# Output projection's first part: the gate scaled by ScalarE on the way out of PSUM, the residual added by a DMA

## The chip, the cores and the metric

The kernel runs on one core of a Trainium2 chip. Its engines have queues of their own: TensorE (PE in the profile, its weight loads PEld), VectorE (DVE), ScalarE (ACT), GpSimd (POOL) and SyncE (SP), which only issues transfers. The metric is the device time of one execution in microseconds, as the median of several runs; less is better.

## The reference, cut to what matters

Two layers run over 640 tokens: 512 latent tokens and 128 context tokens, which have modulation vectors of their own. The part at issue is the gated residual after the mixer:

```
sh1, sc1, gt1, sh2, sc2, gt2 = _modulation(c, w_ada[l], b_ada[l])
h = _rms_norm(xs, g_mix[l]) * (1.0 + sc1) + sh1
mix = _mixer_latent(h, ...)              # concat of window attention, Fourier mixing, latent attention
xs = xs + gt1 * (mix @ w_out[l])
h = _rms_norm(xs, g_ffn[l]) * (1.0 + sc2) + sh2
xs = xs + gt2 * _conv_ffn(h, w_ug[l], conv_w[l], conv_b[l], w_down[l])
```

The context tokens go the same way with `c_ctx`.

## The kernel before, in words

Activations lie transposed: the residual is 8 chunks of 128 features by 640 tokens, a chunk to a tile `x` of 320 KB. Each matmul in float32r is done three times (high times high, low times high, high times low), so weights and activations are split into a high part, made by ScalarE (`wh`, `mh`, `CK`, ...: line 125), and a low part, made by VectorE (`wl`: line 188, `ml` and the like: line 144).

A layer is a mixer (projections, attention, output projection) and a feed-forward part, whose matmuls are dense. In the mixer, attention units run in a pipeline, and a generator called `filler` gives TensorE other work between them, in an order written by hand in `CFG[l]["order"]`: projections, the Fourier part, the parts of the latent attention, the modulation vectors of layer 0 (`early`, `ada`) and the steps `po0` to `po3`. The order on each engine is then set by a scheduler from this program order; an engine runs its own list strictly in order.

`po0` to `po3` are the first part of the output projection, two chunks each. The generator `part1` multiplies those input features that are ready early (4 of 8 blocks, or 6 of 8 for `po3` of layer 1) and leaves residual plus gated partial sum in DRAM, in `xpart[l]`. For that it loads the old residual chunk into a tile `xp` from `xsrc` (the input `xT` in layer 0, the buffer `xd` in layer 1), lets VectorE add the gated product in PSUM to it (`resid`, line 537: three instructions a chunk, over 320, 192 and 128 columns, since the two kinds of token have gates of their own), and stores it. `gate` is a copy of one column by GpSimd, which holds back what GpSimd issues next.

`pre_tail`, called with the fourth latent-attention unit, loads the eight sums from `xpart` into the tiles `x`; these loads stand behind the last store on GpSimd's queue. The second part multiplies the blocks left over and adds them to `x` with `resid`, whose `x` rows begin a layer's last mixer stretch; then the feed-forward part follows.

Three resources around this matter. PSUM has two large accumulators (the pool `pmm`, tiles `mm`) and four small ones (`pss`, tiles `s`). `part1` uses a large one for chunks 0 to 3 and small ones for 4 to 7 (`wide`); the attention scores, the key projection `knope` and others use the large ones too, in turn. SBUF tiles of most kinds come from one pool of 54 buffers. Weight tiles `wr` have two buffers (`NWR`): unit i+2 is loaded by SP when unit i has been split, that is, after its `wl` row on VectorE. The blocks `wa` of the modulation matrix are loaded by SP as well (line 301) and multiplied at line 320; the sums go through ScalarE (`adasb`) and a transpose (line 330).

```
            self.nsp = i + 1
            self.load_to(i + 2)
```

Of the kernel before, what the change touches and what calls it, by code (L numbers as in the profile page):

```python
# [10 lines left out]
AF = mybir.ActivationFunctionType  # L11
ALU = mybir.AluOpType
# [9 lines left out]
HF = 320  # L22
# [51 lines left out]
def segs(hf):  # L74
    return [(0, 320, 0)] if hf == 0 else [(320, 512, 0), (512, 640, 1)]
# [3 lines left out]
def hybrid_step(ctx: ExitStack, tc: tile.TileContext, I, O):  # L79
    nc = tc.nc  # L80
# [9 lines left out]
    def S(name, dt=F32, w=NT):  # L90
        return sp.tile([128, w], dt, tag="S", name=name)
# [23 lines left out]
    def SM(name, w=4, bufs=4):  # L115
        return sm.tile([128, w], F32, tag=name, name=name, bufs=bufs)
# [137 lines left out]
    mod = [const.tile([128, 48, 2], F32, name=f"mod{l}") for l in range(L)]  # L254
    amod = [const.tile([128, 2, 8, 2], F32, name=f"amod{l}") for l in range(L)]
    xd = dr.tile([8, 128, NT], F32, name="xd")
    xpart = [dr.tile([8, 128, NT], F32, name=f"xpart{l}") for l in range(L)]
# [15 lines left out]
    def dense(w, hs, ks, ps, first, last, hfs=(0, 1), off=0, n=NT, fix=False):  # L273
        for k in ks:
            for pi, (wi, hi) in enumerate(((0, 0), (0, 1), (1, 0))):
                for hf in hfs:
                    c0, c1 = hf * HF, n if hf else HF
                    pin(nc.tensor.matmul(  # L278
                        ps.h[hf][:, :c1 - c0], lhsT=w[wi][:, off[k] if isinstance(off, dict) else k + off, :], rhs=hs[hi][k][:, c0:c1],
                        start=(first and k == ks[0] and pi == 0), stop=(last and k == ks[-1] and pi == 2),  # L280
                    ), fix)
            yield 0.41 * len(hfs)
# [250 lines left out]
    def resid(xc, ps, l, gidx, c, hfs):  # L533
        for hf in hfs:
            for c0, c1, v in segs(hf):
                o = c0 - hf * HF
                nc.vector.scalar_tensor_tensor(  # L537
                    out=xc[:, c0:c1], in0=ps.h[hf][:, o:o + c1 - c0], scalar=mod[l][:, gidx * 8 + c, v:v + 1],
                    in1=xc[:, c0:c1], op0=ALU.mult, op1=ALU.add)
# [108 lines left out]
    def gate(t):  # L648

        g = SM("gate", 1)  # L650
        last_gate[0] = nc.gpsimd.tensor_copy(g, t)

    def gated(ins):
        if last_gate[0] is not None:
            tc.keep_in_program_order(ins)
        return ins
# [14 lines left out]
    def mixer(l, norm, begun, xsrc):  # L671
# [261 lines left out]
        def part1(i):  # L933
            late = i in CFG[l]["late"]
            while st["a"] < (10 if late else 5):
                yield 1e9
            for c in (2 * i, 2 * i + 1):
                xt = S("xp")
                gated(nc.gpsimd.dma_start(out=xt, in_=xsrc[c]))
                ps = Acc(c < CFG[l]["wide"])  # L940
                n = 6 if late else 4
                yield from dense(W.get(u["o", c if late else 2 * i]), (mh, ml), KORD[:n], ps, True, True, off={k: j + (0 if late else n * (c % 2)) for j, k in enumerate(KORD[:n])})
                resid(xt, ps, l, 2, c, (0, 1))
                nc.gpsimd.dma_start(out=xpart[l][c], in_=xt)
                gate(xt[:, 0:1])
                yield 0.0

        def filler():
            mla()
            parts = dict(fourier=fourier(*dft), q2=one("q2", cb_q(2)), q3=one("q3", cb_q(3)), kv=kv(), k1=k1())  # L950
            parts.update(zip(("ckv", "cqA", "cqB", "rest"), st["parts"]))
            parts.update({f"po{i}": part1(i) for i in range(4)})
            early = ada_pe(l, (4, 5) if l == 0 else (), CFG[l]["ahead"][0])
            ada = ada_pe(l, range(6, 10) if l == 0 else (), CFG[l]["ahead"][1])
            for n in CFG[l]["order"].split():
                if n == "load":
                    next(ada, None)
                elif n in ("early", "ada"):
                    yield from ada_chunk(early if n == "early" else ada)
                else:  # L960
                    if n == "ckv":
                        rope_load("ropeC")
                    yield from parts[n]
            for v in ada:
                yield max(v, 0.0)
# [219 lines left out]
        xn = {}  # L1185
        def pre_tail():
            for c in range(8):
                xn[c] = S("x")
                gated(nc.gpsimd.dma_start(out=xn[c], in_=xpart[l][c]))

        def pre_g1():
            while 7 not in Q:
# [26 lines left out]
        for c in range(8):  # L1219
            ps = Acc()  # L1220
# [8 lines left out]
    if True:  # L1229
# [22 lines left out]
        for l in range(L):  # L1252
# [8 lines left out]
            xn, nrm = mixer(l, nrm, begun, I["xT"] if l == 0 else xd)  # L1261
# [70 lines left out]
            for kind, a in u["plan"]:  # L1332
                if kind == "up":
                    for q, cb in (("a", cb_a(a)), ("g", cb_g(a))):
                        ps = Acc()
# [12 lines left out]
                if not last:  # L1348
                    for c in range(8):
                        ps = Acc()  # L1350
# [3 lines left out]
                else:  # L1354
# [7 lines left out]
                    ps = Acc()  # L1362
# [144 lines left out]
```

## Time and profile before

| what | value |
|---|---|
| median of 3 runs | 1579.41 us (1579.19 to 1580.35) |
| the profiled execution's own time | 1573.21 us |
| span of its profile | 1571.4 us, 25819 instructions |
| PE busy | 1516.5 us (97%) |
| DVE busy | 1116.8 us (71%) |
| ACT busy | 712.1 us (45%) |
| POOL busy | 103.3 us (7%) |

The span is the profiled execution from its first to its last instruction; its own time has 1.8 us around it, and the median of the other runs lies 6.2 us higher. A share of busy time is a mean over stages with different limits.

### The profile page before, as it was taken

The numbers are of one execution on the slowest core, as the hardware profiler recorded it, in microseconds if no ns is written. First come the engines' busy times: TensorE is split into PE (matmuls) and PEld (weight loads), VectorE is DVE, ScalarE is ACT, GpSimd is POOL, SyncE is SP. The second block draws the span as 40 slices with busy tenths as digits, with TensorE's granted clock in tenths as the row PEclk, the third lists the DMA queues.
The fourth block names the chain that finished last, engine by engine and source line by source line (L and its number), as shares of the span: only waits on it lengthen the run. The fifth ranks groups of instructions, "written<-read, shape, count | busy, mean of one in ns | idle before, by whom it ended". The sixth has DMA issues, their size and how long they took to land. (4 is left out here: it accounts for less than half of the span.)

```text
span 1571.4 us, 25819 instructions
## 1 busy us (share of the span) xinstructions
PE 1516.5 (97%) x10082; PEld 1420.1 (90%) x10082; DVE 1116.8 (71%) x2257; ACT 712.1 (45%) x1401; POOL 103.3 (7%) x225
## 2 busy tenths in 40 slices
PE   9999989899999999999989999989999999999997
PEld 7977775599999999999989887869999999999996
DVE  5765684478896887888788777867885466466366
ACT  4555674564432432441445666656433243244142
POOL 1200111100000000001011001120000000000000
PEclk9999999999999999999999999999999999999999
DMA  9542238113334335325334202331332212221311
GB/s 366 174 138 74 73 106 308 54 68 108 121 135 148 103 122 184 108 92 209 100 139 130 77 23 88 115 143 68 108 108 68 93 62 63 92 78 53 99 54 67
DMA packets 61800, 177.59 MB, mean 113 GB/s; under 512 B 7360, under 2 KB 9856, under 8 KB 61680
## 3 DMA queue, kind: packets, MB, share of 16 engines
q1 hardware_dynamic: 44112, 116.41, 22.5%
q0 software_dynamic: 17568, 59.55, 11.1%
q8 instruction: 79, 1.29, 0.3%
q14 instruction: 41, 0.34, 0.1%
HBM read 165.02 MB, written 10.91 MB: 112 GB/s over the span
## 5 line engine op out<-in xcount | busy, mean ns | idle before, releaser
L278 PE MATMUL mm<-hh,wh 128*128 128x320 f32 x1632 | 378.0, 312 | 8.0 <-ACT u L125 6.2
L278 PE MATMUL mm<-hl,wh 128*128 128x320 f32 x1632 | 377.4, 310 | 0.9 <-DVE hl L469 0.5
L278 PE MATMUL mm<-hh,wl 128*128 128x320 f32 x1632 | 377.2, 310 | 0.0
L125 ACT ACTIVATE wh<-wr 128x1024 fp32r<-128x1024 f32 (+2 forms) x189 | 185.9, 984 | 332.0 <-PE mm L278 253.1
L278 PEld LDWEIGHTS mm<-hh,wh 128*128 128x128 f32 x1632 | 273.8, 188 | 15.8 <-ACT u L125 7.6
L278 PEld LDWEIGHTS mm<-hl,wh 128*128 128x128 f32 x1632 | 275.5, 188 | 4.2 <-issue 2.1
L278 PEld LDWEIGHTS mm<-hh,wl 128*128 128x128 f32 x1632 | 274.1, 188 | 3.3 <-issue 3.3
L188 DVE TENSOR_TENSOR wl<-wr,wh 128x1024 fp32r<-128x1024 f32 (+2 forms) x187 | 210.9, 1128 | 45.9 <-ACT wh L125 44.8
L1288 DVE SCALAR_TENSOR_TENSOR y<-u,pk,y 128x642 f32<-128x642 f32 x176 | 156.1, 887 | 64.1 <-ACT y L1285 60.2
L278 PE MATMUL mm<-th,wh 128*128 128x320 f32 x624 | 142.4, 310 | 0.8 <-DVE x L537 0.8
L278 PE MATMUL mm<-tl,wh 128*128 128x320 f32 x624 | 142.3, 309 | 0.0
L278 PE MATMUL mm<-th,wl 128*128 128x320 f32 x624 | 142.3, 309 | 0.0
L1285 ACT ACTIVATE y<-u,bb,pk 128x513 f32<-128x513 f32 (+1 forms) x176 | 105.9, 650 | 58.2 <-DVE bb L1282 58.2
L364 DVE CUSTOM_DVE_ANT_0 junk<-wa,sbc 128x1024 bf16<-128x1024 f32 x112 | 131.9, 1222 | 0.4 <-DMA wa<-in_wat 0.4
L537 DVE SCALAR_TENSOR_TENSOR x<-mm,mod,x 128x320 f32<-128x320 f32 (+2 forms) x210 | 80.1, 435 | 70.7 <-PE mm L278 70.6
L1278 DVE TENSOR_TENSOR u<-mm,r 128x512 f32<-128x512 f32 (+1 forms) x176 | 79.9, 486 | 47.6 <-PE mm L278 45.5
L278 PEld LDWEIGHTS mm<-th,wh 128*128 128x128 f32 x624 | 104.2, 188 | 1.6 <-issue 1.0
L278 PEld LDWEIGHTS mm<-tl,wh 128*128 128x128 f32 x624 | 104.4, 188 | 0.1
L278 PEld LDWEIGHTS mm<-th,wl 128*128 128x128 f32 x624 | 104.4, 188 | 0.0
L125 ACT ACTIVATE u<-mm 128x2 f32<-128x2 f32 x176 | 20.8, 170 | 124.1 <-DVE u L1278 123.7
L361 POOL DMA_DIRECT2D wa<-in_wat x56 | 29.5, 528 | 563.6 <-DVE mod L364 556.9
L1302 ACT ACTIVATE y<-y 128x642 f32<-128x642 f32 x44 | 32.6, 741 | 73.7 <-DVE y L1288 73.7
(310 smaller groups left out, 2232.1 us busy)
## 6 DMA issues: line engine op xcount, KB each, us to landing
wr<-in_wug SPq DMA_DIRECT2D x88, 512.0 KB, 3.5
wa<-in_wat POOLq DMA_DIRECT2D x56, 512.0 KB, 3.7
wa<-in_wa SPq DMA_DIRECT2D x80, 256.0 KB, 5.4
wr<-in_wdn SPq DMA_DIRECT2D x48, 384.0 KB, 3.1
wr<-in_wi SPq DMA_DIRECT2D x16, 512.0 KB, 3.7
wr<-in_wo SPq DMA_DIRECT2D x14, 512.0 KB, 3.7
xpart<-xp POOLq DMA_DIRECT2D x16, 320.0 KB, 3.8
x<-xpart POOLq DMA_DIRECT2D x16, 320.0 KB, 7.7
```

Source lines behind the costliest of these rows:

```text
L125: return nc.scalar.activation(out, in_, AF.Copy)
L188: pin(self.eng.tensor_sub(lo, r, f32(hi)), fix)
L278: pin(nc.tensor.matmul(ps.h[hf][:, :c1 - c0], lhsT=w[wi][:, off[k] if isinstance(off, dict) else k + off, :], rhs=hs[hi][k][:, c0:c1], sta ...
L361: nc.gpsimd.dma_start(out=t, in_=I["wat"][i0 + i])
L364: nc.vector.tensor_tensor_reduce(out=junk, in0=t, in1=sb[v], scale=1.0, scalar=0.0, op0=ALU.mult, op1=ALU.add, accum_out=mod[l][:, n, v:v ...
L537: nc.vector.scalar_tensor_tensor(out=xc[:, c0:c1], in0=ps.h[hf][:, o:o + c1 - c0], scalar=mod[l][:, gidx * 8 + c, v:v + 1], in1=xc[:, c0:c ...
L1278: nc.vector.tensor_mul(halves(uu[:, p:p + n]), ps.t[:, :, o:o + n // 2], halves(nrm.r[:, c0:c1]))
L1285: nc.scalar.activation(y[:, c0:c1], uu[:, c0 + 1:c1 + 1], AF.Identity, bias=bb[:, v:v + 1], scale=cv[:, t, 1:2])
L1288: nc.vector.scalar_tensor_tensor(out=yy, in0=uu[:, q:q + TW], scalar=cv[:, t, q:q + 1], in1=yy, op0=ALU.mult, op1=ALU.add)
L1302: nc.scalar.activation(y, y, AF.Silu)
```

## The change

`part1` no longer loads the residual. After its matmuls ScalarE writes gate times product from PSUM into `xp`, in the same three pieces as VectorE did (a copy with a scale of one value a partition), and GpSimd issues the store. The `gate` after it is gone. `pre_tail` loads the eight old residual chunks into the tiles `x`, and then issues eight transfers from `xpart` into the same tiles that add in place of overwriting. The count of GpSimd's transfers stays: per layer 8 loads `xp`, 8 stores and 8 loads `x` become 8 stores, 8 loads and 8 adding transfers.

```
-                xt = S("xp")
-                gated(nc.gpsimd.dma_start(out=xt, in_=xsrc[c]))
                 ps = Acc(c < CFG[l]["wide"])
                 n = 6 if late else 4
...
-                resid(xt, ps, l, 2, c, (0, 1))
+                xt = S("xp")
+                for hf in range(2):
+                    for c0, c1, v in segs(hf):
+                        o = c0 - hf * HF
+                        nc.scalar.activation(xt[:, c0:c1], ps.h[hf][:, o:o + c1 - c0], AF.Copy, scale=mod[l][:, 16 + c, v:v + 1])
                 nc.gpsimd.dma_start(out=xpart[l][c], in_=xt)
-                gate(xt[:, 0:1])
                 yield 0.0
...
             for c in range(8):
                 xn[c] = S("x")
-                gated(nc.gpsimd.dma_start(out=xn[c], in_=xpart[l][c]))
+                gated(nc.gpsimd.dma_start(out=xn[c], in_=xsrc[c]))
+            for c in range(8):
+                nc.gpsimd.dma_start(out=xn[c], in_=xpart[l][c], accum_op=ALU.add)
```

The scheduler gives other lists to the engines. Three places follow; line numbers from 946 on are one higher in the changed kernel.

The first is SP in layer 0's mixer, from the load of the key weights `wukv` on (`wo` are output-projection weights, `wa` modulation blocks, `wug` weights of the feed-forward part). Before:

```order
L168 DMA wr<-in_wukv 128x512
L301 DMA wa<-in_wa 128x512 x4
L168 DMA wr<-in_wo 128x2x512 x5
L301 DMA wa<-in_wa 128x512 x16
L168 DMA wr<-in_wo 128x2x512
L301 DMA wa<-in_wa 128x512 x12
L168 DMA wr<-in_wug 128x1024 x14
```

With the change:

```order
L168 DMA wr<-in_wukv 128x512
L301 DMA wa<-in_wa 128x512 x4
L168 DMA wr<-in_wo 128x2x512 x6
L301 DMA wa<-in_wa 128x512 x28
L168 DMA wr<-in_wug 128x1024 x14
```

The sixth load of `wo` has moved ahead of sixteen loads of `wa`.

The second is ScalarE in layer 0 where the first latent keys are split (`krc`, `CK`, `CKX`), after two copies of transposed attention weights `PT`. Before:

```order
L125 ACTIVATE PT<-s 128x512 x2
L125 ACTIVATE krc<-krf 32x512
L125 ACTIVATE CK<-mm 64x640
L1028 ACTIVATE P,den<-P,negm 128x384 x2
L125 ACTIVATE CKX<-krf 32x128
L1028 ACTIVATE P,den<-P,negm 128x384
L125 ACTIVATE CKX<-mm 64x128
```

With the change:

```order
L125 ACTIVATE PT<-s 128x512 x2
L945 ACTIVATE xp<-mm,mod_86 128x320
L945 ACTIVATE xp<-mm,mod_86 128x192
L945 ACTIVATE xp<-mm,mod_86 128x128
L125 ACTIVATE krc<-krf 32x512
L1029 ACTIVATE P,den<-P,negm 128x384
L125 ACTIVATE CK<-mm 64x640
L1029 ACTIVATE P,den<-P,negm 128x384
L125 ACTIVATE CKX<-krf 32x128
```

The evacuation of chunk 3 now stands ahead of the key split.

The third is ScalarE some 40 us later, where the second pair of latent keys (`CKb`, `CKX`) leaves its large accumulator; before it stand two copies `PT`. Before:

```order
L1113 ACTIVATE P<-P,den 128x640 x2
L125 ACTIVATE wh<-wr 128x1024
L125 ACTIVATE CKb<-mm 64x640
L125 ACTIVATE wh<-wr 128x1024
L125 ACTIVATE CKb<-CK 32x640
L125 ACTIVATE CKX<-mm 64x128
L125 ACTIVATE adasb<-s 128x512
L125 ACTIVATE CKb<-mm 64x640
L125 ACTIVATE CKX<-mm 64x128
```

With the change:

```order
L125 ACTIVATE CKb<-mm 64x640
L945 ACTIVATE xp<-s,mod_86 128x320
L945 ACTIVATE xp<-s,mod_86 128x192
L945 ACTIVATE xp<-s,mod_86 128x128
L125 ACTIVATE CKb<-CK 32x640
L125 ACTIVATE CKX<-mm 64x128
L1114 ACTIVATE P<-P,den 128x640
L125 ACTIVATE CKb<-mm 64x640
L945 ACTIVATE xp<-s,mod_86 128x320
L945 ACTIVATE xp<-s,mod_86 128x192
L945 ACTIVATE xp<-s,mod_86 128x128
L1114 ACTIVATE P<-P,den 128x640
```

Right behind that come `CKX`, two `wh` and `adasb`. Both `P` rows, the two `wh` and `adasb` have moved behind the two evacuations. On TensorE the score products of `CKb`, which stood behind the sums of `wa` (line 320), now stand between them: four sums, six score products, two sums, five score products.

## Rows read from the trace of the kernel before

**Rows 1.** The page's part 1: busy time, share of the span, instructions.

```profile
PE 1516.5 (97%) x10082; PEld 1420.1 (90%) x10082; DVE 1116.8 (71%) x2257; ACT 712.1 (45%) x1401; POOL 103.3 (7%) x225
```

**Rows 2.** Windows: start:end, length, busy us of PE, PEld, DVE, ACT, POOL, clock, DMA, GB/s.

```profile
172.00:258.00 86.00, 78.54 (x482) 61.68 (x482) 56.78 (x148) 52.33 (x109) 10.89 (x27) 0.94 0.47 158
...
941.00:1023.00 82.00, 77.16 (x497) 65.74 (x496) 66.67 (x163) 53.28 (x115) 11.28 (x27) 0.98 0.32 97
```

**Rows 3.** The tile xp: durations min/median/max in ns, first and last start, forms.

```profile
L537 DVE SCALAR_TENSOR_TENSOR xp<-mm,mod,xp x24: 340/408/551, 172.8 to 982.9; 128x320 f32<-128x320 f32 x8, 128x192 f32<-128x192 f32 x8, 128x128 f32<-128x128 f32 x8
L537 DVE SCALAR_TENSOR_TENSOR xp<-s,mod,xp x24: 340/410/551, 227.5 to 1021.9; 128x320 f32<-128x320 f32 x8, 128x192 f32<-128x192 f32 x8, 128x128 f32<-128x128 f32 x8
...
DMA to landing us min/median/max: 2.5/3.5/5.9
```

**Rows 4.** Groups by form on ScalarE: count, busy us, mean ns, idle before.

```profile
L125 ACT ACTIVATE mh<-s 128x128 fp32r<-128x128 f32 x40 | 10.9, 273 | 9.1 <-PE s L979 5.7 <-DVE ml L144 3.1
...
L516 ACT ACTIVATE hh<-x,amod 128x128 fp32r<-128x128 f32 x16 | 6.2, 387 | 0.0
...
L125 ACT ACTIVATE CKb<-mm 64x640 fp32r<-64x640 f32 x4 | 2.8, 690 | 0.4 <-DVE CKX L144 0.3
...
L125 ACT ACTIVATE fb<-mm 128x386 f32<-128x386 f32 x4 | 1.9, 482 | 0.1
```

**Rows 5.** Timeline of SP's queue: start, us from first to last, what.

```profile
220.57 20.56 SPq L301 DMA_DIRECT2D wa<-in_wa  x16
241.46 0.38 SPq L168 DMA_DIRECT2D wr<-in_wo  x1
```

**Rows 6.** Timeline of VectorE: start, us, what.

```profile
234.31 1.21 DVE L188 TENSOR_TENSOR wl<-wr,wh 128x1024 fp32r<-128x1024 f32 x1
```

**Rows 7.** Timeline of TensorE, the same columns; an f32 matmul shows as two records.

```profile
238.19 1.06 PE L320 MATMUL s<-wa,sT 128*32 128x512 f32 x8
...
240.63 3.88 PE L320 MATMUL s<-wa,sT 128*32 128x512 f32 x16
```

**Rows 8.** Windows, columns as in rows 2.

```profile
240.00:245.00 5.00, 4.47 (x20) 1.26 (x20) 0.36 (x2) 0.40 (x1) 0.07 (x1) 1.00 1.05 405
```

**Rows 9.** Timelines of TensorE and ScalarE at the first keys.

```profile
223.06 0.36 PE L286 MATMUL mm<-wh,CX 128*128 128x256 f32 x1 [1.08 <-DVE den L1032]
...
221.78 0.26 ACT L125 ACTIVATE CKX<-mm 64x128 fp32r<-64x128 f32 x1
```

**Rows 10.** Timelines of ScalarE, VectorE and TensorE at the second keys.

```profile
254.89 1.56 ACT L1113 ACTIVATE P<-P,den 128x640 f32<-128x640 f32 x2
...
263.55 0.29 DVE L144 TENSOR_TENSOR CKX<-mm,CKX 64x128 fp32r<-64x128 f32 x1
...
257.12 1.92 PE L320 MATMUL s<-wa,sT 128*32 128x512 f32 x14
...
271.19 1.00 PE L286 MATMUL mm<-CKb,CQ 96*128 96x320 f32 x5
```

**Rows 11.** Waits of TensorE from 941 to 1023 us: total us, times, longest.

```profile
PE s L1047 <- DVE PT L134: 0.9, 1, 0.9
PE s L1122 <- DVE xp L537: 0.9, 1, 0.9
PE mm L286 <- ACT P L1101: 0.8, 1, 0.8
```

**Rows 12.** Transfers x: GpSimd's timelines, landing in layer 1, VectorE's first use there.

```profile
263.21 3.17 POOL L1189 DMA_DIRECT2D x<-xpart  x6 [0.39 <-DMA wr<-in_wug]
...
1023.04 4.45 POOL L1189 DMA_DIRECT2D x<-xpart  x8
...
x<-xpart POOLq DMA_DIRECT2D x8, 320.0 KB, 8.5
...
1060.65 1.14 DVE L537 SCALAR_TENSOR_TENSOR x<-mm,mod,x 128x320 f32<-128x320 f32 x3 [0.98 <-PE mm L278]
```

**Rows 13.** Windows, columns as in rows 2.

```profile
202.00:204.00 2.00, 2.00 (x9) 2.00 (x8) 1.97 (x4) 0.63 (x1) 0.00 (x0) 0.50 0.00 0
```

## Prediction

> **What bounds the kernel now.** I read the page's busy shares first: TensorE is busy for 1516.5 of 1571.4 us [rows 1], so the whole kernel has 55 us in which it does nothing, and an edit that neither shortens TensorE's own work nor takes such a pause away gains nothing, however much it relieves VectorE (71%). Next I cut out the two stretches in which the first part of the output projection runs, one a layer. TensorE is busy for 78.5 of 86 us in the first and for 77.2 of 82 in the second [rows 2]: 7.5 and 4.8 us idle. VectorE has 57 and 67 us of work there, ScalarE 52 and 53. So the two are nearly equally loaded in layer 0, and VectorE is clearly the fuller one in layer 1. Last I read who was waited for in layer 1's stretch: VectorE's PT copies once for 0.9 us, a transpose behind an xp row for 0.9, and ScalarE's P, itself behind VectorE's maxima, for 0.8 [rows 11].
>
> **What is removed.** VectorE loses 24 instructions a layer, 340 to 551 ns each, median about 410 [rows 3]: some 10 us. GpSimd loses eight waits of its gate and has as many transfers as before. That can shorten the end only where TensorE waits for VectorE. In layer 1 the three waits add up to 0.9 + 0.9 + 0.8 = 2.6 us [rows 11]. I take 2.0, because one of them also needs ScalarE, which gets longer; the ends are 0 and 2.6. In layer 0 I take no gain: its one wait of this kind, 1.08 us at 223.06 [rows 9], is the one that the next paragraphs lengthen.
>
> **What ScalarE gets.** No row shows a scaled copy from PSUM over these widths. The nearest are fb, 386 columns from PSUM without a scale operand, 482 ns; mh, 128 columns from PSUM, 273 ns; and hh, 128 columns from SBUF with the same kind of scale operand, 387 ns [rows 4]. The first two give 0.81 ns a column, so 428, 325 and 273 ns, 1.03 us a chunk. With the 114 ns between mh and hh added three times it is 1.37 us. I take 1.2, near the upper end since the operand is there and neighbours overlap a little; eight chunks are 9.6 us a layer. Most of that stands where ScalarE pauses. It costs only where TensorE waits for a row behind it, and the new order shows two such places in layer 0.
>
> The Trainium skill ("ScalarE: Activation LUTs", section "Rules for kernel authors") says to multiply on VectorE and not on ScalarE, with up to a factor of 3 for it in bf16. The rows here are fp32: 387 ns on ScalarE stand against 340 on VectorE at 128 columns. By the rule a chunk would cost 3.6 us and the two places below about three times as much; I go by the rows.
>
> At the first keys the evacuation of chunk 3 stands ahead of krc, CK and CKX. TensorE's next product waits there for a large accumulator, at 223.06, after ScalarE's last CKX at 221.78 [rows 9]. The group of 1.2 us delays that CKX, and VectorE's relief comes too early in this alternation to give it all back: +0.9 us, ends 0 and 1.2.
>
> At the second keys two evacuations and the P pair now stand ahead of the last CKX. The PT copies before end at 254.89, when the P pair (1.56 us) began [rows 10]. From there the new list needs three times 0.69 for two CKb from PSUM and one of like length from SBUF, two groups of 1.2, the 1.56 of the P pair and two CKX of 0.26 [rows 4, 9, 10]: 2.1 + 2.4 + 1.6 + 0.5 = 6.6, so 261.5, and VectorE's own CKX behind it makes about 262. Only then is that large accumulator free for the second score product of the next unit. Before, it was free at 263.8 and wanted at 271.19, so it cost nothing [rows 10]. Now the scores stand between the sums of wa. From 257.12 TensorE has four sums, a score product and two sums ahead of it, about 1 us each, the score's from the row of 1.00 [rows 10], the sums' about as the eight records of 1.06 [rows 7]: it comes there at 260.2 and waits. +2.0 us, ends 0 (if those evacuations turn out earlier) and 3.5 (adasb, now behind two wh, late as well).
>
> **What SP's order costs.** This is the term of which the diff says nothing. Before, sixteen loads of wa went out from 220.57 on, and the sixth wo after them at 241.46 [rows 5]. That wo has to wait for the split of the unit two places ahead, whose wl row ended at 234.31 + 1.21 = 235.52 [rows 6]; before, it had long been free when its turn came. Now it stands ahead of all 28 wa, and SP cannot get past it before 235.5. The first four wa behind it feed the sums at 238.19, the next eight those that ended at 240.63 + 3.88 = 244.51 [rows 7]. Transfers ran at 405 GB/s around there [rows 8]. One wo and twelve wa are 0.52 + 3.15 = 3.67 MB, 9.1 us at that rate. A chunk of 0.33 MB landed at best 2.5 us after its issue [rows 3], 0.8 of it bytes, so about 1.7 are added: 235.5 + 9.1 + 1.7 = 246.3, which is 1.8 us late. A store of xp in the same time adds up to 0.8. I take +2.2; the ends are 0 (the waits on their buffers had held the wa back just as long) and 3.8 (the split a group of 1.2 us later too). Nothing hides it: the sums stand in TensorE's order, and the adding of chunks 6 and 7 comes behind them.
>
> **What the adding transfers cost.** They and the loads before them stand on GpSimd behind the last store. In layer 1 the eight loads were issued from 1023.04 in 4.45 us and landed 8.5 us after issue; the first use was at 1060.65 [rows 12]. Eight adding transfers more, each behind its load, make 1024 + 4.5 + 4.5 + 8.5 = 1041.5 if an add costs as much as a load: 19 us of cover, nothing added. Layer 0 issued from 263 [rows 12] and has more. No row shows an adding transfer: its lower end is the plain one, its upper end I leave to a rival.
>
> **The sum.** +2.2 (SP) + 0.9 (first keys) + 2.0 (second keys) − 2.0 (VectorE in layer 1) = +3.1 us, 1576.3 for the profiled execution's own 1573.21. That execution is 6.2 us below the median of the runs shown, so I give the difference to the median: 1582.5 us.
>
> **The rivals.** *VectorE's relief decides* (faster): the three costs are hidden, the buffers held the wa as long as SP does now, and the keys come in time because VectorE, half of their alternation, is earlier. Then 2.6 us come in layer 1 and the 1.08 at 223.06 with them [rows 9, 11]: −3.7, 1575.7. For it speaks that layer 1's VectorE is at 67 of 82 us; against it that no wait named there is long. It decides if each of the three costs stays under 1 us.
>
> *Nothing moves*: every wait taken away turns into one of like length on ScalarE, and SP's wait is covered: 1579.4.
>
> *The adding transfers are late*: if each takes 5 us, one after the other, eight of them end at 1028 + 40 = 1068, 8 us after VectorE wants the first chunk, and the feed-forward part starts that much later: 1587. It decides from about 4 us each on. The Trainium skill ("DMA: Bandwidth & Descriptors", section "SDMA does more than copy") puts such adds into units inside the data stream, which speaks for the price of a plain transfer; no run here shows it yet, and the chance of this rival is low with or without it.
>
> *The clock falls as well*: from 202 to 204 us TensorE was granted half its clock, the lower of its two levels, after a pause of some 3.7 us [rows 13]. Two new pauses of 2 us could each be followed by a stretch like that, 3 us at half speed, 1.5 lost each: 1585.5.
>
> **How the numbers follow.** The forecast's case, costs in layer 0 larger than the gain in layer 1, has a chance of 0.54, with a range of its own from 1579.5 to 1585.5. VectorE's relief gets 0.19, nothing moves 0.10, late adds 0.08, the clock 0.09. A measurement of this kernel can tell about 0.2%, 3.2 us. The forecast lies at that line, so its case splits in about equal halves: slower 0.28 + 0.08 + 0.09 = 0.45, same 0.26 + 0.10 = 0.36, faster 0.19. The range goes from 1575.5, the relief's case, to 1587, the late adds.
>
> **What the changed profile would show.** ScalarE's xp rows at 1.0 to 1.4 us a chunk. SP's first wa after about 235, and a wait of TensorE's sums on wa of 2 us or more around 238 to 246. A pause of TensorE before the second score product of CKb, ended by a CKX. No wait for an xp row around 1020. Adding transfers landed well before 1060. The prediction is wrong if the wa land as early as before, if the xp rows on ScalarE sit in its pauses at both key splits, or if the adds take several times a plain transfer.

## The result, and the profile after

The changed kernel takes 1604.75 us (median of 4 runs, 1601.53 to 1607.99), the kernel before 1579.3 us on the same chip (4 runs, 1579.16 to 1580.35). The ratio is 1.0156, with a 95% interval from 1.0137 to 1.0175: 25 us slower, far above the forecast of 1582.5 and outside its range of 1575.5 to 1587. The profiled execution took 1607.99 us, the slowest of the four; its span is 1606.2 us, 34.8 more than in the profile before.

The page's first part of the changed kernel:

```profile
PE 1538.2 (96%) x10082; PEld 1434.1 (89%) x10082; DVE 1100.8 (69%) x2209; ACT 727.3 (45%) x1449; POOL 105.7 (7%) x209
```

Against [rows 1] TensorE is busy 21.7 us longer with the same 10082 instructions, and idle for 1606.2 − 1538.2 = 68.0 us where it was 54.9. The loss is thus 13.1 us of pauses and 21.7 us in which the same matmuls took longer. VectorE got 16.0 us shorter and ScalarE 15.2 longer, where the prediction had some 20 and 19.

This pair of profiles shows more than the medians do, 34.8 us against 25. A part of that is not the change: in the first 30 us, where no engine's list differs yet, the changed kernel's execution already had a lower clock (0.89, the second row, against 1.00), which makes 3.3 us.

```profile
0.00:30.00 30.00, 27.14 (x187) 22.07 (x188) 15.30 (x32) 15.81 (x25) 4.37 (x8) 1.00 0.97 357
0.00:30.00 30.00, 25.70 (x170) 20.16 (x170) 11.79 (x26) 12.36 (x19) 4.38 (x8) 0.89 0.96 354
```

The two mixer stretches of the changed kernel, cut at the same work as [rows 2] (columns as there):

```profile
175.00:276.00 101.00, 89.47 (x493) 67.37 (x491) 52.89 (x133) 61.20 (x136) 6.14 (x12) 0.90 0.34 120
962.00:1053.00 91.00, 79.57 (x496) 68.96 (x496) 58.89 (x141) 59.27 (x135) 5.59 (x11) 0.92 0.21 68
```

They last 101 and 91 us where they lasted 86 and 82. About as many matmul records stand in them, but the granted clock is 0.90 and 0.92 (0.94 and 0.98 before), and TensorE pauses for 11.5 us in each. Both layers lose, layer 1 too, where the prediction had expected a gain.

TensorE's waits of the whole span, of the changed kernel (total us, times, longest):

```profile
PE mm L286 <- ACT P L1102: 10.3, 9, 2.0
...
PE mm L286 <- DVE CKX L144: 2.9, 2, 2.6
...
PE s L330 <- ACT adasb L125: 2.8, 4, 0.7
...
PE s L320 <- DMA wa<-in_wa: 1.3, 2, 1.0
...
PE mm L278 <- ACT xp L945: 0.2, 1, 0.2
```

The same view of the kernel before:

```profile
PE mm L286 <- ACT P L1101: 4.9, 5, 2.0
...
PE s L330 <- ACT adasb L125: 1.5, 2, 0.8
```

The largest new item is the first: key and score products (line 286) want a large accumulator that ScalarE's exponential `P` has not yet read out. The only row that names `xp` has 0.2 us. To see where the waits on `P` come from, here is TensorE in layer 1 at the first latent scores, in the changed kernel:

```profile
1012.74 0.45 PE L278 MATMUL s<-mh,wl 128*128 128x320 f32 x2
1015.79 0.36 PE L286 MATMUL mm<-wh,CX 128*128 128x256 f32 x1 [2.60 <-DVE CKX L144]
...
1016.57 2.10 PE L286 MATMUL mm<-CK,CQ 96*128 96x320 f32 x12
1018.50 1.04 PE L1048 MATMUL s<-ident,P 128*128 128x128 f32 x8
1020.84 2.02 PE L286 MATMUL mm<-CK,CQ 96*128 96x320 f32 x12 [1.30 <-ACT P L1102]
1024.90 1.22 PE L286 MATMUL mm<-CL,wh 128*128 128x512 f32 x2 [2.04 <-ACT P L1102]
```

and in the kernel before:

```profile
990.60 0.36 PE L286 MATMUL mm<-wh,CX 128*128 128x256 f32 x1 [0.51 <-DVE CKX L144]
...
991.38 1.05 PE L286 MATMUL mm<-CK,CQ 96*128 96x320 f32 x6
992.27 0.27 PE L1047 MATMUL s<-ident,P 128*128 128x128 f32 x1
992.32 1.15 PE L286 MATMUL mm<-CK,CQ 96*128 96x320 f32 x6
993.31 0.71 PE L1047 MATMUL s<-ident,P 128*128 128x128 f32 x5
994.84 1.14 PE L286 MATMUL mm<-CK,CQ 96*128 96x320 f32 x6 [0.81 <-ACT P L1101]
...
998.76 0.30 PE L278 MATMUL s<-mh,wl 128*128 128x320 f32 x1
999.02 0.73 PE L286 MATMUL mm<-CL,wh 128*128 128x512 f32 x2
```

TensorE's own list is another one. In this stretch the second key product (`mm<-CL,wh`) stood behind twelve projection matmuls and found its accumulator free; now it follows the scores at once and waits 2.04 us. The scores stood in four groups of six with transposes between; now they come in two of twelve. And the clock falls there (windows of the changed kernel, columns as in [rows 2]):

```profile
1014.00:1024.80 10.80, 5.76 (x38) 5.12 (x38) 7.88 (x19) 4.95 (x12) 0.19 (x1) 1.00 0.01 2
1024.80:1028.20 3.40, 3.29 (x12) 2.90 (x13) 1.51 (x4) 1.68 (x5) 0.00 (x0) 0.50 0.00 0
1028.20:1034.00 5.80, 5.80 (x42) 4.94 (x42) 1.34 (x3) 4.71 (x10) 0.56 (x1) 1.00 0.14 57
```

TensorE does 5.76 us of work in 10.8, and then runs at 0.50, the lower of its two levels (1.2 of 2.4 GHz), for 3.4 us. At this place the kernel before has no such stretch.

The clock also falls at the first keys of layer 0. There the product that waits 1.08 us at 223.06 in the kernel before [rows 9] waits 1.83 us at 228.54, and then TensorE works for 6.8 us at 0.50. The first row is of the kernel before, the second of the changed one:

```profile
230.00:250.00 20.00, 18.47 (x121) 12.29 (x121) 9.76 (x26) 9.54 (x20) 1.28 (x4) 1.00 0.88 319
229.50:236.30 6.80, 6.80 (x26) 5.71 (x26) 2.25 (x5) 3.13 (x9) 0.75 (x2) 0.50 0.13 51
```

So 0.75 us more of waiting was followed by a stretch that costs 3.4.

SP's queue in the changed kernel, from the output-projection weights on, which answers to [rows 5]:

```profile
201.44 42.53 SPq L168 DMA_DIRECT2D wr<-in_wo  x3
244.06 27.80 SPq L301 DMA_DIRECT2D wa<-in_wa  x28
```

The third load of `wo` is the sixth of its row; the `wa` behind it leave at 244.06 instead of 220.57. Last, the new operations themselves. The tile `xp` (durations min/median/max in ns, columns as in [rows 3]):

```profile
L945 ACT ACTIVATE xp<-mm,mod x24: 348/422/531, 174.2 to 1006.9; 128x320 f32<-128x320 f32 x8, 128x192 f32<-128x192 f32 x8, 128x128 f32<-128x128 f32 x8
```

The tile `x` in layer 1, with the times to landing of its 16 transfers:

```profile
L1190 POOL DMA_DIRECT2D x<-xd x8: 536/536/541, 1054.5 to 1058.2; - x8
L1192 POOL DMA_DIRECT2D x<-xpart x8: 848/921/971, 1058.7 to 1066.3; - x8
...
DMA to landing us min/median/max: 3.6/8.2/12.2
```

VectorE's first use of `x` there, from its timeline:

```profile
1093.75 1.14 DVE L537 SCALAR_TENSOR_TENSOR x<-mm,mod,x 128x320 f32<-128x320 f32 x3 [0.98 <-PE mm L278]
```

A piece on ScalarE costs 348 to 531 ns, a chunk 1.3 us by the three and less where they overlap. An adding transfer takes GpSimd 921 ns to issue where a plain one takes 536, but the last is issued at 1066.3 and, with the longest time to landing, there by 1078.5: 15 us ahead of the first use.

### The profile page after: what moved, and what is told of

Same layout as the page of the kernel before. It is cut to its first block, busy times and chain, and to the rows that moved or that the text cites. A ratio compares the mean times of both kernels' runs of the same rounds, so it can differ in the third digit from the quotient of the medians.

```text
span 1606.2 us, 25768 instructions
## 1 busy us (share of the span) xinstructions
PE 1538.2 (96%) x10082; PEld 1434.1 (89%) x10082; DVE 1100.8 (69%) x2209; ACT 727.3 (45%) x1449; POOL 105.7 (7%) x209
## 3 DMA queue, kind: packets, MB, share of 16 engines
q0 software_dynamic: 18592, 59.55, 11.5%
## 6 DMA issues: line engine op xcount, KB each, us to landing
x<-xpart POOLq DMA_DIRECT2D x16, 320.0 KB, 10.4
```

## The experiments

Four theories stood at the start or came up on the way (the first expectation of the second section below also names a fifth, that what is missing on GpSimd and SP makes the loss). Theory 1: SP's new order makes the loss. Theory 2: ScalarE's longer queue does. Theory 3: the adding transfers do. Theory 4, formed after the first four runs: TensorE's own new order does.

Every ratio is to the kernel before on the same chip in the same hours; its median was 1576.06 us beside the first four runs, then 1580.02, 1581.16 and 1581.01. Since the clock's share differs from run to run, a second number helps to tell pauses from clock: the span of a run times its mean granted clock, about the time that it would take with the same pauses and all work at full clock. For the changed kernel's four runs it is 1606.2 × 0.978 = 1570.9, 1571.9, 1571.6 and 1572.6; for the kernel before its median is between 1554.5 and 1555.4 in all four sets. I call it the time at full clock. The clock is given to 0.001, so rounding alone makes it uncertain by some 0.8 us; and since it counts all time at the lower level as half lost, pauses too, it is rather too low, and the more so the more time lies at that level: pauses have rather more of a loss than it gives them. The ratios and the differences of the medians do not agree in the last tenth of a per cent.

| run | us, median | ratio (95%) | at full clock |
|---|---|---|---|
| changed kernel | 1604.75 | 1.0156 (1.0137 to 1.0175) | 1571.7 |
| e_sp | 1602.73 | 1.0169 (1.0148 to 1.0190) | 1567.5 |
| e_vec | 1611.83 | 1.0222 (1.0205 to 1.0240) | 1576.0 |
| e_noadd | 1605.73 | 1.0188 (1.0167 to 1.0208) | 1570.4 |
| e_l1 | 1588.55 | 1.0069 (1.0038 to 1.0099) | 1557.3 |
| e_l0 | 1593.15 | 1.0090 (1.0061 to 1.0119) | 1566.7 |
| e_pe_rev | 1594.78 | 1.0100 (1.0067 to 1.0133) | 1566.5 |
| e_load_vec | 1577.89 | 0.9994 (0.9975 to 1.0013) | 1555.6 |
| e_load_act | 1589.32 | 1.0064 (1.0038 to 1.0089) | 1562.2 |
| e_act_order | 1587.49 | 1.0046 (1.0028 to 1.0064) | 1562.0 |
| e_three | 1590.38 | 1.0066 (1.0049 to 1.0084) | 1561.8 |
| e_key | 1587.69 | 1.0042 (1.0025 to 1.0058) | 1560.2 |
| e_rest | 1596.25 | 1.0099 (1.0080 to 1.0117) | 1566.1 |
| e_block0 | 1583.55 | 1.0021 (1.0006 to 1.0035) | 1556.0 |
| e_pin | 1607.0 | 1.0166 (1.0147 to 1.0186) | 1569.8 |

### One part of the change at a time

**e_sp** gives SP its old order back.

```
+                    if self.nl == 21:
+                        with tc.issue_after(wa_ins[(8, 3)].ins):
+                            d = nc.sync.dma_start(out=o, in_=src)
```

> The changed kernel, with SP's sixth load of wo back behind sixteen wa, as before the change; every other engine keeps the changed list. Theory 1 (SP's order makes the loss of layer 0): the wa go out from about 225 instead of 244, the waits on wa vanish, and 10 to 15 us come back: about 1590 to 1594. Theory 2 (ScalarE's longer queue delays keys and scores): no more than 2 us come back, 1602 to 1605. Theory 3 (adding transfers): as theory 2.

1602.73 us, 3.0 less than e_noadd beside it, whose lists are otherwise those of the changed kernel. SP's queue shows that the mechanism is real:

```profile
223.11 25.08 SPq L307 DMA_DIRECT2D wa<-in_wa  x16
248.45 0.38 SPq L172 DMA_DIRECT2D wr<-in_wo  x1
```

and so does TensorE's wait on `wa` (line numbers here are 6 higher):

```profile
PE s L326 <- DMA wa<-in_wa: 0.4, 1, 0.4
```

The `wa` leave 21 us earlier, and the wait on them shrinks from 1.3 to 0.4 us. But only some 3 us come back, little more than the spread (the runs of the two overlap; at full clock they lie apart, 1567.3 to 1568.3 against 1569.4 to 1572.2): theory 1 explains an eighth of the loss.

**e_vec** lets VectorE scale.

```
-                        nc.scalar.activation(xt[:, c0:c1], ps.h[hf][:, o:o + c1 - c0], AF.Copy, scale=mod[l][:, 16 + c, v:v + 1])
+                        nc.vector.tensor_scalar_mul(xt[:, c0:c1], ps.h[hf][:, o:o + c1 - c0], mod[l][:, 16 + c, v:v + 1])
```

> The changed kernel, but VectorE instead of ScalarE scales the product on its way out of PSUM; SP's and GpSimd's lists are those of the changed kernel. Theory 1 (SP's order): the loss of layer 0 stays, 1595 to 1605. Theory 2 (ScalarE's queue): the loss goes, 1578 to 1585. Theory 3 (adding transfers): the loss stays whole, 1602 to 1606.

1611.83 us, above what any theory gave: with the load gone and GpSimd's and SP's lists those of the change, the loss stays without ScalarE's pieces, and the kernel is 6 us slower than e_noadd. But TensorE's list is neither that of before nor that of the changed kernel here, so the run does not clear ScalarE by itself. Its waits (as above):

```profile
PE mm L286 <- ACT P L1102: 12.0, 10, 2.1
PE mm L286 <- DVE CKX L144: 6.8, 3, 2.8
```

The wait on `P` is longer still. So it needs no `xp` on ScalarE.

**e_noadd** leaves out the old residual.

```
-                gated(nc.gpsimd.dma_start(out=xn[c], in_=xsrc[c]))
-            for c in range(8):
-                nc.gpsimd.dma_start(out=xn[c], in_=xpart[l][c], accum_op=ALU.add)
+                gated(nc.gpsimd.dma_start(out=xn[c], in_=xpart[l][c]))
```

> The changed kernel without the adding transfers: the tiles x are loaded from xpart alone, as before the change, so the old residual is left out of the sum. The lists of TensorE, VectorE, ScalarE and SP are those of the changed kernel. Theories 1 and 2: 1601 to 1606, as the changed kernel. Theory 3 (the adding transfers, at 0.8 to 1.2 us an issue and about 10 us to land, make the loss): 1580 to 1592.

1605.73 us. Theory 3 is out.

**e_l1 and e_l0** make the change in one layer and keep the old `part1` and `pre_tail` in the other.

```
+                if l != 1:
+                    xt = S("xp")
+                    gated(nc.gpsimd.dma_start(out=xt, in_=xsrc[c]))
...
+                if l != 1:
+                    resid(xt, ps, l, 2, c, (0, 1))
+                else:
...
```

> The change in layer 1 alone; layer 0 has the first part of the kernel before. In the profile the changed kernel lost 16.7 us between 190 and 290 us (layer 0) and 12.4 us between 940 and 1061 us (layer 1). If the two are independent: 1579 + 9 to 12 = 1588 to 1591. If layer 1's loss comes from the state that layer 0 left behind (the clock, late loads): 1579 to 1583.

> The change in layer 0 alone; layer 1 has the first part of the kernel before. The change in layer 1 alone cost 12.5 us, the whole change 25 us. If the two add up: 1588 to 1592.

1588.55 us with layer 1 alone, 12.5 more than before, and 1593.15 us with layer 0 alone, 13.1 more: together 25.6, the whole loss (by the ratios 0.69% and 0.90%). At full clock layer 1 alone loses about 2 us and layer 0 alone about 12. So a large part of layer 1's loss is clock, but not all but 2 us of it: in e_l1's profiled execution TensorE is idle for 1591.7 − 1529.6 = 62.1 us, 7.2 more than in the profile before.

### TensorE's order

After these runs the slow kernels had one thing in common: TensorE's list. In e_sp and e_noadd it is that of the changed kernel word for word, and e_vec has one of its own that is nearer to it than to the old one. It differs from the list before in 20 stretches, nine in layer 0 and eleven in layer 1. One of them, the first scores of layer 1, before the change:

```
L286 MATMUL mm<-CK,CQ 128x320 x6
L1047 MATMUL s<-ident,P 128x128
L286 MATMUL mm<-CK,CQ 128x320 x6
L1047 MATMUL s<-ident,P 128x128 x5
L286 MATMUL mm<-CK,CQ 128x320 x6
L1047 MATMUL s<-ident,P 128x128
L286 MATMUL mm<-CK,CQ 128x320 x6
L1047 MATMUL s<-ident,P 128x128 x3
```

and with it:

```
L286 MATMUL mm<-CK,CQ 128x320 x12
L1048 MATMUL s<-ident,P 128x128 x8
L286 MATMUL mm<-CK,CQ 128x320 x12
L286 MATMUL mm<-CL,wh 128x512 x2
L286 MATMUL mm<-CL,wl 128x512
L1048 MATMUL s<-ident,P 128x128 x4
```

Both kernels give TensorE the same 9641 matmuls in the same program order, so one kernel can be made to follow the other's list, by edges that fix only the order of issue on the engine named (numbers of instructions in program order, as start+length; the lists are cut here):

```
+ORDER["PE"] = "0+261 267+5 261+6 272+1 276+12 ..."
...
+        for a, b in zip(want, want[1:]):
+            tc.add_manual_dep(
+                made[b], made[a].name,
+                mybir.DependencyInfo(mybir.DependencyClass.NoSync, mybir.DependencyReason.DATA),
+                reason="follow")
```

**e_pe_rev**: the kernel before, with TensorE's list of after and no edited instruction of the change. SP's and GpSimd's lists are those of before. ScalarE's and VectorE's are not quite: the scheduler orders them anew around the given list, and 15 and 31 of their instructions stand elsewhere. At the second keys, for instance, ScalarE now copies a `CKb` (259.43) ahead of the `P` pair, which stood first before [rows 10].

> The kernel before (residual loaded, VectorE's sum, no adding transfers), with one thing of the change: TensorE issues its matmuls in the order of the changed kernel; SP's and GpSimd's lists are those of before. Theory 4 (the loss comes from the new order of TensorE's list, in which score and key products stand close behind each other and the fill work between them is gone): 1590 to 1602. Theory 5 (the loss comes from what is missing on GpSimd and SP: other loads, other times of the buffers): 1576 to 1581.

1594.78 us, 14.8 more than before, 11 of them at full clock. Theory 4 holds for the larger part, if TensorE's list is taken with what the scheduler moves along with it; no run tells the two apart. Theory 5 is out for this part, since GpSimd and SP have here all that they had before. The waits are those of the changed kernel (line numbers 17 higher):

```profile
PE mm L303 <- ACT P L1118: 11.5, 10, 2.4
...
PE s L347 <- ACT adasb L142: 2.9, 4, 0.8
...
PE mm L303 <- DVE CKX L161: 1.3, 1, 1.3
```

**e_load_vec**: the reverse, as nearly as it could be had. With the load into `xp` and the `gate` kept (what was loaded is overwritten) and VectorE scaling, the scheduler gives TensorE, ScalarE and SP the lists of the kernel before; the adding transfers stay. Against the kernel before:

```
-                resid(xt, ps, l, 2, c, (0, 1))
+                for hf in range(2):
+                    for c0, c1, v in segs(hf):
+                        o = c0 - hf * HF
+                        nc.vector.tensor_scalar_mul(xt[:, c0:c1], ps.h[hf][:, o:o + c1 - c0], mod[l][:, 16 + c, v:v + 1])
...
-                gated(nc.gpsimd.dma_start(out=xn[c], in_=xpart[l][c]))
+                gated(nc.gpsimd.dma_start(out=xn[c], in_=xsrc[c]))
+            for c in range(8):
+                nc.gpsimd.dma_start(out=xn[c], in_=xpart[l][c], accum_op=ALU.add)
```

> The changed kernel, with the load of the old residual into xp and the gate kept (the loaded values are overwritten) and VectorE scaling in place of ScalarE. TensorE's, ScalarE's and SP's lists are then word for word those of the kernel before; only the adding transfers and a scaled copy in place of the sum on VectorE are left of the change. Theory 4: 1576 to 1581, as before. Theory 3 (adding transfers) in full: over 1595; half of it: about 1588.

1577.89 us, ratio 0.9994: the adding transfers are free, and with the old list the loss is gone. The wait on `P` is that of before:

```profile
PE mm L286 <- ACT P L1104: 4.9, 5, 2.0
```

No run gives the changed kernel itself TensorE's list of before.

**e_key, e_rest, e_pin, e_block0** look for the move that matters. e_key moves only the second key product, in the kernel before; e_rest has the rest of the new list without that move; e_pin pins that product in the changed kernel; e_block0 has only the coarser blocks of scores in layer 0. All but e_pin are edited against the kernel before by `ORDER["PE"]` alone, with what the scheduler then moves: 10 instructions of ScalarE and 12 of VectorE in e_key, 12 and 32 (and 2 of SP) in e_rest, none and 1 in e_block0. e_pin differs from the changed kernel by this in `knope`, with the product's other matmuls written out behind it:

```
+                first = nc.tensor.matmul(ps[:, 0, :], lhsT=wk[0][:, 0, m * 128:(m + 1) * 128], rhs=CL[0], start=True, stop=False)
+                pin(first, m == 1)
```

> The kernel before, with one move in TensorE's list a layer: the six matmuls of the second key product stand, as in the changed kernel, right behind the scores and their transposes, ahead of the projection matmuls that stood before them. The changed kernel waits 1.17 us there in layer 0 and 2.04 us in layer 1 for an accumulator. If such waits are the loss and the clock falls after each (3.4 us at half speed, 1.7 lost): 2 to 6 us more than before, 1581 to 1586. If the whole of the new order is needed: within 2 us of before.

> The kernel before with TensorE's list of the changed kernel, but the second key product back behind the projection matmuls. The whole list cost 14.8 us. If the two moves of the key product are the main part of it: 1581 to 1586. If it is the scores and transposes standing in blocks instead of alternating: 1588 to 1594.

> The changed kernel with the second key product pinned behind the projection matmuls in both layers; the rest of its lists stays nearly the same. If the key product's waits carry the loss: 1590 to 1598. If not: 1600 to 1606.

> The kernel before, with one piece of the new order of TensorE in layer 0 alone: the projection matmuls, the transposes and the first scores of the keys stand in blocks (10 scores, 8 transposes, 8 projection matmuls, 6 scores) where they alternated more finely. If the blocks carry the loss of layer 0 (7 us in the profile of the kernel before with the whole new list): 1583 to 1588. If not: within 2 us of before.

The key product alone costs 0.42% (6.5 us between the medians, 5 at full clock), a little above the upper end that I gave it. TensorE's wait on `P` in e_key:

```profile
PE mm L303 <- ACT P L1118: 8.3, 8, 2.1
```

But e_rest is as slow as the whole list (1.0099 against 1.0100), and pinning the product in the changed kernel gives nothing back (1.0166 against 1.0156). The same wait in e_rest:

```profile
PE mm L303 <- ACT P L1118: 6.0, 6, 2.0
```

It is 5.5 us shorter than in e_pe_rev, yet TensorE is idle for 1592.1 − 1528.7 = 63.4 us of the span, against 64.7 in e_pe_rev and 54.9 before: other, smaller waits have taken its place. The blocks of layer 0 cost 0.2%, between the two expectations; that run also has all of the edges, so the edges themselves do not cost more than about that. So neither of these moves carries the loss; take the key product's away, and the rest still makes it up.

### ScalarE's pieces with the order held

**e_load_act** is e_load_vec with ScalarE scaling (the line of e_vec, reversed). TensorE gets a third list by it. **e_act_order** makes TensorE and SP follow the lists of before, and **e_three** VectorE as well, without the 48 sums that it no longer has:

```
+ORDER["PE"] = "0+261 267+5 261+6 272+1 276+12 ..."
+ORDER["SP"] = "0+51 67+2 73+1 51+16 ..."
+ORDER["DVE"] = "0+2 98+1 468+2 2+68 ..."
```

> As the kernel with the kept load and gate and VectorE's scaling, but ScalarE scales. TensorE's list is then neither that of before nor that of the changed kernel; SP's is that of before. If ScalarE's three pieces a chunk cost what the prediction gave them, about 3 us: 1579 to 1584. If any list but the tuned one loses: 1590 to 1605.

> ScalarE scales, the load of the old residual and the gate are kept, the adding transfers are there, and TensorE and SP follow the lists of the kernel before word for word. Against the same kernel with its own order (TensorE's list another one, 9.3 us slower than before). Theory 4 (TensorE's list): 1577 to 1583. Theory 2 (ScalarE's pieces stand in the way of keys and scores): 1586 to 1592.

> ScalarE scales, the load and the gate are kept, the adding transfers are there; TensorE, SP and now VectorE too follow the lists of the kernel before (VectorE's without the 48 sums that ScalarE has taken over). With TensorE's and SP's lists alone it was 6 to 7 us slower than before. If that rest was VectorE's own new order: 1577 to 1583. If it is ScalarE's longer list (P and PT behind the xp pieces): 1585 to 1591.

1589.32, 1587.49 and 1590.38 us: 0.64%, 0.46% and 0.66% more than before, and 7 us each at full clock. So with the old order ScalarE's evacuation does cost something, where VectorE's costs nothing (e_load_vec), and neither TensorE's nor VectorE's list explains it. ScalarE's own list is not held: in e_three 16 of its other instructions stand elsewhere too. e_three's waits:

```profile
PE s L349 <- ACT adasb L144: 3.0, 3, 1.4
...
PE s L1069 <- ACT PT L144: 2.3, 2, 1.6
...
PE mm L305 <- DVE CKX L163: 1.5, 1, 1.5
...
PE s L1144 <- ACT xp L965: 0.8, 1, 0.8
```

The sums of `wa` wait 3.0 us for ScalarE (1.5 before), transposes 2.3 us for its `PT` (0.6 before), and a key product 1.5 us for `CKX` (0.5 before). These three make 4.2 us of the 7; I don't put the rest down to single rows.

## Why the prediction was wrong

*What bounds the kernel.* That TensorE's pauses in the two stretches decide was right. What failed is the step from there to the sum: but for one place, the prediction costed each changed instruction within TensorE's old order. It read the new lists of SP and ScalarE at three places and TensorE's at one, the score products of `CKb`, and TensorE's had changed in 20 stretches. That list, with what the scheduler moves on ScalarE and VectorE to fit it, costs 14.8 us without any edited instruction (e_pe_rev), more than all the terms of the sum together, and no term stood for it.

*VectorE's relief in layer 1, −2.0 us.* This is the term with the wrong sign. VectorE did get shorter, 58.9 us in layer 1's stretch where it had 66.7, but TensorE's waits on it there grew, from 4.0 to 6.5 us, and those on ScalarE's `P` from 0.8 to 4.7. Only the wait for `xp` fell, from 0.9 to 0.2. Layer 1's part of the change costs 12.5 us (e_l1). The starting point was read short as well: [rows 11] has three of the six waits of that stretch, 2.6 of 4.8 us. And in layer 0 the wait at 223.06 is not the only one for VectorE; another, 3.67 us for `CQ` at 200.34, is 3.7 in the changed kernel too, so leaving it out cost the sum nothing.

*SP's order, +2.2 us (0 to 3.8).* Right in mechanism and about in size: 3.0 us between e_noadd and e_sp. The split that the sixth `wo` has to wait for ended at 243.58, not 235.52, since the whole stretch had slipped, and the `wa` left at 244.06. The waits on `wa` are 1.3 us, where 2 or more were forecast.

*First keys, +0.9 us.* Right for the wait, which is 0.75 us longer; the 6.8 us at 0.50 behind it, 3.4 us more, were in no term.

*Second keys, +2.0 us.* Not seen: the score product of `CKb` waits 0.26 us at 276.06 for `CKX`. The sums of `wa` ahead of it were late themselves, which probably hid it.

*ScalarE's price, 1.2 us a chunk.* Right: 348 to 531 ns a piece, 1.07 us for three that follow each other in e_three. VectorE's scaled copy took 339 to 552 ns in e_load_vec, so a piece has the same price on either engine; yet with TensorE's order held ScalarE's pieces cost 7 us at full clock and VectorE's nothing. The Trainium skill ("ScalarE: Activation LUTs", section "Rules for kernel authors") says to multiply on VectorE; the price of the piece does not bear it out here, the kernel's time does.

*The adding transfers, nothing.* Right (e_noadd, e_load_vec). They land 15 us ahead of their use where I gave 19.

*The rivals.* VectorE's relief, nothing moves and late adds are out. The clock was named, and priced at 3 us. It gave more: of the 25 us some 16 to 17 are there at full clock (1571.7 against 1554.5 to 1555.4), which leaves 8 to 9, or somewhat less, to the clock. In the pair of profiles it is more: the clock's mean fell from 0.991 to 0.978, which over the two spans is 1606.2 × 0.022 − 1571.4 × 0.009 = 21.2 us, and TensorE was busy 21.7 us longer. But that pair is an extreme one, since the kernel before had clocks of 0.982 to 0.990 beside the experiments. In e_l1's profile the same sum gives 20.9 us, and TensorE was busy only 13.1 us longer. The Trainium skill ("TensorE: Matmul & The Clock Gate", section "Terms") gives "Penalty ≈ this × (1 − K/N)" for the time at the lower level, half of that time here; the changed kernel's profile agrees, e_l1's stays below it.

*What stays open.* How the shares add up. TensorE's order, with what moves along with it on ScalarE and VectorE, makes 14.8 us, ScalarE's pieces 6 to 9, SP 3, and the sum of these is near 25; but with the load dropped VectorE's scaling is slower than ScalarE's (e_vec), so they are not independent, and the agreement may be chance. Which of TensorE's moves matter stays open too: no single one of those tried carries the loss. Why the scheduler makes another list of it I have only from the lists: keeping the load restores the old one with VectorE's scaling and not with ScalarE's.

No kernel tried was faster than the one before; e_load_vec equals it.

## What to carry to other kernels

When an edit changes what a list scheduler sees, compare the list of the engine that bounds the kernel first, above all if the edit does not touch it; the costs of the edited instructions come second. The same matmuls in another order can cost more than the edit itself, and making the old kernel follow the new list is a run that shows it without the edit. Compare the other engines' lists in that run too, since the scheduler fits them to the one that is held. Look also at the clock behind each new pause: here 0.75 us more of waiting was followed by a stretch that cost 3.4.

## What was not expected of the hardware

Clock and pauses: three waits of 2.60, 1.30 and 2.04 us in 11 us were followed by 3.4 us at half clock, though TensorE worked between them. The first keys show it with less: one wait of 1.83 us, then 6.8 us at half clock, where the kernel before waits 1.08 us and keeps 1.00. The Trainium skill ("TensorE: Matmul & The Clock Gate", section "A second HAM failure mode: psum-queue depth-cycling") tells of a bf16 kernel whose clock went up and down over short idle times between groups of matmuls; the windows above show the like in fp32r.

Adding transfers: in layer 1 GpSimd issues one in 848 to 971 ns against 536 to 541 for a plain load of the same 320 KB, and such a transfer landed a median of 10.4 us after its issue in the whole of the changed kernel, with each waiting for the load of its tile.
